# Joining the 64-column runs, and all 512 tokens channels first: one layer of a hybrid encoder on one core

## The chip, the cores and the metric

The kernel runs on one core of a Trainium2 chip. A core has TensorE (PE, matrix products), VectorE (DVE), ScalarE (ACT), GpSimd (POOL) and SyncE (SP, which here only issues transfers), with on-chip memory (SBUF) and accumulators for the products (PSUM, eight banks). The metric is the device time of one execution in microseconds; lower is better.

## The reference

One encoder layer on 512 tokens of 1024 channels. Its first half mixes tokens, its second half is an MLP.

```python
h = rmsnorm(x, pre_mix_norm[l])
proj = h @ w_in[l]
z, xbc, dt_raw, q, k, v, gates = split_cols(proj, IN_SPLITS)
y_ssd = ssd_branch(z, xbc, dt_raw, ...)            # 8 groups of 4 heads, both directions, 4 chunks of 128
y_attn = window_attention(q, k, v, attn_sink[l], rel_bias_table) @ w_attn_out[l]   # 16 heads, +-128 tokens
g = jax.nn.sigmoid((gates + b_gate[l]).astype(jnp.float32))
mixed = (g_ssd * y_ssd + g_attn * y_attn) @ w_o[l]
x = x + rmsnorm(mixed, post_mix_norm[l])
h = rmsnorm(x, pre_mlp_norm[l])
f = jnp.square(jax.nn.relu(h @ w_mlp_in[l])) @ w_mlp_out[l]
x = x + rmsnorm(f, post_mlp_norm[l])
```

`rmsnorm` divides a token's row by the root of its mean square and multiplies each channel by a gain. The row's factor can therefore be applied after a product, since it is one number for each token.

## The kernel before, in words

All data are float32. Most products are made in three parts: a weight `w` and an operand `h` are each split into a high part that TensorE takes in its fast format (fp32r) and a low remainder, and `mm3` adds high x high, high x low and low x high. ScalarE makes the high parts (L513 for weights), GpSimd and VectorE the low ones (L517 for weights, always on GpSimd there). A few products stay in plain fp32.

The program is a list of quanta, each one block of 128 output columns with its weight loads (`cm`, 24 products of 512 columns for a block with 8 parts). Actions between quanta (attention heads, SSD steps) are put at places in that list. All instructions are then recorded and reordered by `Planner`, a list scheduler with a table of costs: it writes a fixed order for each engine, and each engine runs its own queue in that order. A weight tile passes three rings of three buffers: raw (`wr`), high (`wh`) and low (`wl`).

The parts that the change and the prediction touch:

- **The opening** (`start`, `v_quanta`, `start_tokens`, `scale_tokens`). Tokens 0 to 255 come in channels first (`xt`), are multiplied by the gain (`xg`, L685 and L687) and give V and dt by plain products from unnormalised data; the row factor `rst0` is applied when they are taken from PSUM (L617, L618). Tokens 256 to 511 come in token first (`x`), are scaled, transposed by TensorE (L442) and split (L463, L464), and give V and dt by `mm3`. All four blocks of `x` are also read for their sums of squares (L711, L712; L714 and L715 make `rst0`). For tokens 0 to 255 a product of ones with a diagonal of `rst0` (`dg`, L725) spreads the factors over all channels, and L731 to L734 make the split operand `h`. Every later product, K first, reads `h`.
- **Attention** (`attn_scores`, `attn_flip`, `attn_values`). Each head has four blocks of masked scores `P`, their transposes `pT`, and for two heads together 20 products with V whose output fills 64 columns of the array, `ps<-pT,V`.
- **SSD** (`ssd_steps`). For each of 8 groups, `outs(j)` for j = 0 and 1 (two chunks each) makes products of the entering state with C (`ps<-C,pv`), then 8 products of masks with x of 64 columns each (`ps<-m,x`), and merges them on VectorE and GpSimd (L1199 to L1212). `rms` sums squares over channels (`ps<-sh,ones_r`), sends the row through memory and back as a column (`rrow`, `rcol`, `rstd`) and `finish` makes two rows of `yT`.
- **The mixer's output** (`split_y`, `ssd_out_quanta`, `ssd_out_done`, `combine`). 14 of 16 parts of the first two output blocks are multiplied first, and the last two parts, which need the last group, afterwards.

Changing between products of 128 and of 64 columns is a change of TensorE's mode; the planner's `change` knows it, and its `awaited` table lets a 64-column product start only when all that its run needs is ready.

## Time and profile before

| what | value |
|---|---|
| median of 3 runs | 1078.82 us (1078.32 to 1078.97) |
| profiled execution | 1078.3 us, its span 1076.5 us |
| TensorE busy | 1066.9 us, 99% of the span |
| GpSimd, VectorE, ScalarE busy | 798.3, 761.2, 655.5 us |
| granted TensorE clock | 0.998 |
| moved by DMA | 133.21 MB |

The span is the time from the first to the last instruction. In a group of instructions `xN` counts records, and a plain fp32 product leaves two. `out<-in` names the tiles without their buffer numbers. A busy TensorE is not one at its peak, since its instructions overlap and their ends are modelled; starts are the surer reading.

### The profile page before, as it was taken

Reading aid. Unit: us, or ns where it says so; the run is one execution under the profiler, and the core shown is the slowest. Engines: PE = TensorE matmul, PEld = TensorE weight load, DVE = VectorE, ACT = ScalarE, POOL = GpSimd, SP = SyncE. Lnnn points to the kernel's source line nnn. Section 1 sums busy time; section 2 is a strip of 40 time slices with the busy share of each in tenths; the row PEclk is TensorE's granted clock in tenths of the full one; section 3 lists DMA queues with packets and bytes.
Section 4 is the critical chain, followed back from the end, with each engine's and each line's share of the span. In section 5 each row is a group of like instructions: output and inputs, shape, how many; then the busy total and the mean of one; then the engine's idle time right before and its main releaser. Section 6 shows DMA issues by size and latency. Waiting matters only on the chain.

```text
span 1076.5 us, 16682 instructions
## 1 busy us (share of the span) xinstructions
PE 1066.9 (99%) x5542; PEld 895.6 (83%) x5542; DVE 761.2 (71%) x1363; ACT 655.5 (61%) x1409; POOL 798.3 (74%) x991
## 2 busy tenths in 40 slices
PE   9999999999999999999999999999999999999997
PEld 7888888888888888888888888889888888888885
DVE  5777787797787788787778543698663574574698
ACT  7756786777686867676769432456555444444552
POOL 5846558467668899988998965215587898898994
PEclk9999999999999999999999999999999999999999
DMA  8334423433434535243554544317321431424222
GB/s 284 117 101 118 119 81 116 130 101 113 122 112 130 152 113 170 95 151 116 156 140 150 167 146 137 108 52 263 98 69 61 155 98 59 157 94 151 70 98 78
DMA packets 61382, 133.21 MB, mean 124 GB/s; under 512 B 9064, under 2 KB 18792, under 8 KB 61296
## 3 DMA queue, kind: packets, MB, share of 16 engines
q1 hardware_dynamic: 61008, 131.76, 39.3%
q8 instruction: 43, 0.70, 0.3%
q10 hardware_dynamic: 288, 0.39, 0.1%
q14 instruction: 43, 0.35, 0.1%
HBM read 127.63 MB, written 4.49 MB: 123 GB/s over the span
## 4 chain that ended last, share of the span: by engine, by line
PE 96%; DVE 1%; DMA 1%; issue 0%; ACT 0%; POOL 0%; SPq 0%; POOLq 0%; DVEq 0%
PE pp L438 66%; PE ps L438 27%; PE ps L442 3%; DMA wr<-in_wv 1%; PE pp L442 0%; DVE P L940 0%; DVE x L1385 0%; DVE acc L1364 0%; SPq L678 0%; DVE wl L608 0%; DVE ag L1664 0%; DVE h L1372 0%; POOLq L1747 0%; ACT wh L605 0%; POOL mrs L1378 0%
## 5 line engine op out<-in xcount | busy, mean ns | idle before, releaser
L517 POOL TENSOR_TENSOR wl<-wr,wh 128x256 fp32r<-128x256 f32 (+1 forms) x517 | 417.3, 837 | 179.8 <-ACT wh L513 176.4
L438 PE MATMUL pp<-h,wh 128*128 128x512 f32 (+1 forms) x1728 | 525.7, 386 | 0.0
L438 PEld LDWEIGHTS pp<-h,wh 128*128 128x128 f32 x1728 | 318.3, 188 | 61.9 <-issue 1.2
L438 PE MATMUL pp<-h,wl 128*128 128x512 f32 (+1 forms) x864 | 333.7, 386 | 0.0
L513 ACT CAST wh<-wr 128x1024 fp32r<-128x1024 f32 x130 | 135.3, 1041 | 120.6 <-PE pp L438 105.9
L438 PEld LDWEIGHTS pp<-h,wl 128*128 128x128 f32 x864 | 162.6, 188 | 31.8 <-issue 0.2
L1590 POOL TENSOR_TENSOR wl<-wd,wh 128x256 fp32r<-128x256 f32 x158 | 130.7, 864 | 11.8 <-ACT wh L1587 11.8
L1587 ACT CAST wh<-wd 128x512 fp32r<-128x512 f32 x92 | 53.2, 618 | 38.4 <-PE pp L438 19.8
L438 PE MATMUL ps<-wl,fh 128*128 128x512 f32 x184 | 71.8, 390 | 0.0
L438 PE MATMUL ps<-wh,fl 128*128 128x512 f32 x184 | 71.7, 390 | 0.0
L438 PE MATMUL ps<-wh,fh 128*128 128x512 f32 x184 | 71.7, 390 | 0.0
L1425 DVE SCALAR_TENSOR_TENSOR pp<-pp,r 128x256 f32<-128x256 f32 (+1 forms) x31 | 17.3, 559 | 66.1 <-ACT r L1422 65.9
L1168 ACT ACTIVATE n<-cb,tables 128x128 f32<-128x128 f32 x128 | 49.3, 391 | 20.6 <-DVE cb L1159 15.2
L1002 DVE SCALAR_TENSOR_TENSOR u<-pp,cv,u 128x510 f32<-128x510 f32 (+1 forms) x64 | 47.7, 746 | 7.0 <-ACT u L998 5.8
L1169 ACT ACTIVATE m<-cb,tables 128x128 f32<-128x128 f32 x128 | 48.9, 388 | 3.8 <-DVE cb L1159 3.6
L438 PE MATMUL pp<-yl,wh 128*128 128x512 f32 x128 | 49.7, 390 | 0.0
L438 PE MATMUL pp<-yh,wl 128*128 128x512 f32 x128 | 49.7, 389 | 0.0
L438 PE MATMUL pp<-yh,wh 128*128 128x512 f32 x128 | 49.5, 390 | 0.0
L1164 ACT ACTIVATE rf<-rf,tables 128x128 f32<-128x128 f32 x128 | 42.5, 392 | 6.6 <-DMA rf<-csT 6.6
L934 ACT ACTIVATE P<-P,mx 128x384 f32<-128x384 f32 (+1 forms) x64 | 35.2, 553 | 15.9 <-DVE mx L931 15.8
L1204 POOL TENSOR_TENSOR w<-w,E 128x256 f32<-128x256 f32 x48 | 38.7, 820 | 7.6 <-DVE w L1200 6.4
L1100 POOL TENSOR_TENSOR xd<-x,tables 128x256 f32<-128x256 f32 x48 | 32.5, 695 | 15.8 <-ACT x L1025 12.8
(279 smaller groups left out, 2160.1 us busy)
## 6 DMA issues: line engine op xcount, KB each, us to landing
wr<-in_w_in_b SPq DMA_DIRECT2D x74, 512.0 KB, 4.0
wr<-in_w_mlp_in_b SPq DMA_DIRECT2D x32, 512.0 KB, 3.5
wd<-in_w_mlp_out SPq DMA_DIRECT2D x64, 256.0 KB, 4.6
rf<-csT SPq DMA_DIRECT2D x32, 256.0 KB, 4.0
rb<-csT SPq DMA_DIRECT2D x32, 256.0 KB, 4.2
wr<-in_w_ssd_out_b SPq DMA_DIRECT2D x14, 512.0 KB, 3.6
x<-in_x SPq DMA_DIRECT2D x16, 256.0 KB, 5.1
E<-csE SPq DMA_DIRECT2D x32, 128.0 KB, 4.6
```

Source lines behind the costliest of these rows:

```text
L438: self.nc.tensor.matmul(out, lhsT, rhs, start=start, stop=stop, skip_group_check=more)
L513: self.nc.scalar.copy(hi[:, :m], raw)
L517: engines[e].tensor_tensor(lo[:, c], raw[:, c], hi[:, c].bitcast(F32), op=ALU.subtract)
L934: nc.scalar.activation(p[:, :w], p[:, :w], AF.Exp, bias=mx[:, n:n + 1], accum_out=sm[:, n:n + 1])
L1002: nc.vector.scalar_tensor_tensor(u[:, a:e], ps[:, a + d:e + d], self.wtap(t, b), u[:, a:e], op0=ALU.mult, op1=ALU.add)
L1100: nc.gpsimd.tensor_tensor(v4(xd[:, d * 256:(d + 1) * 256]), v4(xs(c)), by_dir(self.coef, c)[:, d].unsqueeze(2).to_broadcast([128, 4, 64]), ...
L1164: nc.scalar.activation(v4(rf)[:, h], v4(rf)[:, h], AF.Identity, bias=ncs[:, 0, h:h + 1])
L1168: nc.scalar.activation(v4(n)[:, h], cb[:, 0], AF.Copy, scale=dt[:, 0, h:h + 1])
L1169: nc.scalar.activation(v4(m)[:, h], cb[:, 1], AF.Copy, scale=dt[:, 1, h:h + 1])
L1204: nc.gpsimd.tensor_tensor(wc, wc, E[:, d], op=ALU.add)
L1587: nc.scalar.copy(hi, src)
L1590: (nc.vector if q == 512 else nc.gpsimd).tensor_tensor(lo[:, c], src[:, c], hi[:, c].bitcast(F32), op=ALU.subtract)
```

## The change

- **All 512 tokens are laid out channels first** in a load of 2 MB (eight tiles of 512 columns). Each is multiplied by the gain and split, without the row factor (`hr`). V and dt of all four token blocks come from these: channel block 0 as a plain product, blocks 1 to 7 by `mm3`, in one pass over the channels with four banks open. The row factor is applied at the eviction of V and dt, for all four blocks. The 16 transposes are gone.
- **K** is computed from `hr` too and scaled at its eviction by the spread row factors `rb`, which are now made for four blocks. The normalised `h` is made afterwards from `xt` and the factors, for the other projections. The `x` tiles now serve only for the sums of squares and are loaded behind `xt` and the V/dt weights; the identity is loaded on SP behind the first K weights.
- **64-column runs are joined.** In SSD groups 3, 4, 6 and 7 the masks' products of j = 0 and 1 stand in one run; attention values (but for the last pair of heads) are held back and put ahead of the next SSD run with j = 1, or j = 0 in the groups that are not joined. The planner takes such a run, and not all products into one bank, as the unit that has to be ready.
- **The mixer**: another order of output blocks, three blocks first in place of two, the later blocks in banks of the other pool, `split_y` in three pieces earlier, the last group's `rms` one quantum later. Score and transpose tiles of the fourth token block share a buffer with others.

```diff
-MIX_ORDER = (0, 4, 1, 5, 2, 6, 3, 7)
+MIX_ORDER, MOST = (0, 4, 2, 6, 1, 5, 3, 7), 3
+SPLIT_Y = ((0, 5, 6), (5, 10, 4), (10, 14, 2))
+Y_BANK = ["ps"] * 8
+PAIRS = (1, 0), (2, 3)
+JOINED = (3, 4, 6, 7)
+ALONE = (7,)
-X_CHUNKS = ((0, 1), (1, 3), (3, 5), (5, 7), (7, 8))
+W_CHUNKS = ((0, 1), (1, 2), (2, 5), (5, 8))
+PLAIN, SCALE_AT = 1, 2.5
-LAST = dict(SCAN, prep=(0, 1, 3, 4), outs=(2.5, 5.5), rms=8, finish=10)
+LAST = dict(SCAN, prep=(0, 1, 3, 4), outs=(2.5, 5.5), rms=9, finish=11)
...
+        def product(k0, k1):
+            def run(parts):
+                if k0 == 0:
+                    banks.extend(self.bank("ps") for _ in range(4))
+                raw, wh, wl = parts[0]
+                for k in range(k0, k1):
+                    for t in range(4):
+                        ps = banks[t][:, :320]
+                        if k < PLAIN:
+                            self.mm(ps, self.xg[k][:, tok(t)], raw[:, k - k0], k == 0, k == 7)
+                        else:
+                            hi, lo = self.hr[k]
+                            self.mm3(ps, (hi[:, tok(t)], lo[:, tok(t)]), (wh[:, k - k0], wl[:, k - k0]), k == 0, k == 7)
+                if k1 == 8:
+                    for t in range(4):
+                        done(t, banks[t])
...
+    def raw_tokens(self):
+        for k, x in enumerate(self.xt):
...
+            hi, lo = self.hr[k]
+            self.split_by(hi, lo, x, g)
+        for t in range(4):
+            xt = self.load_tokens(t)
+            self.token_scale(t, xt)
...
+        self.rb = get("rb")
+        nc.scalar.copy(self.rb, rb)
         for k in range(8):
+            x = self.xt[k]
+            hi, lo = self.h[k]
+            nc.vector.scalar_tensor_tensor(x, x, self.gT[:, k:k + 1], rb, op0=ALU.mult, op1=ALU.mult)
             nc.scalar.copy(hi, x)
+            for e, c in ((nc.vector, slice(0, 512)),) if k % 2 else ((nc.gpsimd, slice(0, 256)), (nc.gpsimd, slice(256, 512))):
+                e.tensor_tensor(lo[:, c], x[:, c], hi[:, c].bitcast(F32), op=ALU.subtract)
...
         def k_done(ps):
+            x = get("kf")
+            nc.vector.tensor_tensor(x, ps, self.rb, op=ALU.mult)
...
         def outs(j):
             def run():
+                off(j)
+                if j == 0 and g in JOINED:
+                    scaled(0)
+                    return
+                while self.due:
+                    self.attn_values(self.due.pop(0))
+                js = (0, 1) if g in JOINED else (j,)
+                for i in js:
+                    diag(i)
+                scaled(j)
+                for i in js:
+                    joined(i)
```

The order of TensorE's queue shows the opening first. Before, the plain products of the second token block (`xg`) are followed by the transposes (`ident,x`; the lines of code are those of the profile):

```order
L438 MATMUL ps_177<-wr_157,xg_116 128x320 x2
L438 MATMUL ps_178<-wr_157,xg_115 128x320
L438 MATMUL ps_178<-wr_157,xg_116 128x320 x2
L442 MATMUL pp_201<-ident,x_205 128x128
L442 MATMUL pp_202<-ident,x_205 128x128
L442 MATMUL ps_203<-ident,x_205 128x128
```

In the changed program (whose lines count 14 more at this place) the queue opens with the warm-up and four plain products, and the three-part products follow at once, one bank after the other:

```order
L452 MATMUL pp_82<-ones_80 128x128 x8
L452 MATMUL ps_229<-wr_142,xg_132 128x320
L452 MATMUL ps_230<-wr_142,xg_132 128x320
L452 MATMUL ps_231<-wr_142,xg_132 128x320
L452 MATMUL ps_232<-wr_142,xg_132 128x320
L452 MATMUL ps_229<-wh_150,hr_109 128x320
L452 MATMUL ps_229<-wl_151,hr_109 128x320
```

Its seam between V and K: the last V product, four products that spread the row factors (`dg`), and then K from `hr` (`pp_434`):

```order
L452 MATMUL ps_232<-wh_162,hr_122 128x320
L452 MATMUL pp_379<-dg_380,ones_80 128x128
L452 MATMUL pp_379<-dg_383,ones_80 128x128
L452 MATMUL pp_379<-dg_386,ones_80 128x128
L452 MATMUL pp_379<-dg_389,ones_80 128x128
L452 MATMUL pp_434<-hr_107,wh_253 128x512
```

Twelve plain products and all transposes have left the queue, 36 three-part products have come, and the factors' products stand ahead of K, where two of them stood inside V.

GpSimd's queue behind the row factors, before: diagonals, K's first weights (`wl_315`), then the low parts of `h`:

```order
L715 TENSOR_TENSOR rst_79<-rst_79,mhalf 128x1
L725 TENSOR_SCALAR dg_262<-ident,rst_79 128x128
L725 TENSOR_SCALAR dg_265<-ident,rst_79 128x128
L517 TENSOR_TENSOR wl_315<-wr_199,wh_314 128x256 x4
L734 TENSOR_TENSOR h_92<-hf_268,h_91 128x256
L734 TENSOR_TENSOR h_94<-hf_268,h_93 128x256
```

The same place in the changed program: both K weight tiles (`wl_254`, `wl_302`), then `h` in turn with the weights of the first Q block (`wl_425`):

```order
L531 TENSOR_TENSOR wl_254<-wr_249,wh_253 128x256 x4
L531 TENSOR_TENSOR wl_302<-wr_251,wh_301 128x256 x4
L742 TENSOR_TENSOR h_92<-xt_124,h_91 128x256 x2
L531 TENSOR_TENSOR wl_425<-wr_299,wh_424 128x256
L742 TENSOR_TENSOR h_96<-xt_126,h_95 128x256 x2
L531 TENSOR_TENSOR wl_425<-wr_299,wh_424 128x256
```

The diagonals have gone to VectorE, `h` stands behind both K tiles, and half of its low parts are VectorE's now.

The last SSD group on TensorE, before: the run of j = 0 between state products, and the run of j = 1, which stands 78 rows later between projections (`pp_6964`):

```order
L438 MATMUL pp_6774<-h_98,wh_6587 128x512
L438 MATMUL pp_6774<-h_97,wl_6588 128x512
L438 MATMUL ps_6792<-C_6456,pv_6603 128x128 x2
L438 MATMUL ps_6795<-m_6618,x_6384 64x128 x4
L438 MATMUL ps_6795<-m_6706,x_6384 64x128 x4
L438 MATMUL ps_6846<-C_6456,B_6361 128x128
```

```order
L438 MATMUL pp_6964<-h_98,wh_6832 128x512
L438 MATMUL pp_6964<-h_97,wl_6833 128x512
L438 MATMUL ps_6985<-m_6850,x_6394 64x128 x4
L438 MATMUL ps_6985<-m_6909,x_6394 64x128 x4
L438 MATMUL pp_6964<-h_99,wh_6832 128x512
```

And in the changed program one run of 16:

```order
L452 MATMUL pp_6982<-h_102,wh_6830 128x512
L452 MATMUL ps_7003<-m_6615,x_6362 64x128 x4
L452 MATMUL ps_7003<-m_6703,x_6362 64x128 x4
L452 MATMUL ps_7012<-m_6848,x_6372 64x128 x4
L452 MATMUL ps_7012<-m_6927,x_6372 64x128 x4
L452 MATMUL pp_6982<-h_101,wl_6831 128x512
```

Both halves now leave the mode once. Over the whole queue, 23 runs of masks and values in the order before are 13 in the changed one, with the same 288 products.

More of the change, by code (lines that the diff above doesn't have):

```diff
@@ L134, in __init__ @@
         self.kind = [self.matmul_kind(n) if e == "PE" else None for n, e in enumerate(self.eng)]
-        self.awaited, banks = {}, {}
+        self.awaited, n0 = {}, None
+        self.runs, last = [], None
         for n, k in enumerate(self.kind):
-            if k and k[1]:
-                banks.setdefault(self.operands(self.ins[n].outs)[0].tensor.name, []).append(n)
-        for bank in banks.values():
-            needed = set().union(*(self.pre[n] for n in bank)) - set(bank)
-            self.awaited.update((n, needed) for n in bank)
+            if k is None:
+                continue
+            if k[1] and last == n0:
+                self.runs[-1].append(n)
+            elif k[1]:
+                self.runs.append([n])
+            n0 = n
+            last = n if k[1] else None
+        for run in self.runs:
+            needed = set().union(*(self.pre[n] for n in run)) - set(run)
+            self.awaited.update((n, needed) for n in run)
     def matmul_kind(self, n):
@@ L648, in run @@
                     self.dt_math()
-            return run
-        return [Quantum([chunk(*c) for c in V_CHUNKS], plain, 0)] + [Quantum([], rest(c), 1) for c in range(3)]
+            return Quantum([chunk(k0, k1)], run)
+        return [product(*c) for c in V_CHUNKS]
     def start(self):
@@ L688, in start @@
-        put(*xt)
-        for t in range(2):
+        self.xt, self.xg = [get("xt") for _ in range(8)], [get("xg") for _ in range(PLAIN)]
+        for k, x in enumerate(self.xt):
+            nc.sync.dma_start(x, self.d_xt[k])
+        self.at(0, self.raw_tokens)
+        self.row = self.const("row", [128, 176])
+        self.sink = self.row[:, 128:144]
+        self.at(1, lambda: self.bcast_row(self.row, self.d_row, 176))
+        self.at(SCALE_AT, lambda: self.scale_tokens(ones))
+        self.at(1, self.later_constants)
@@ L1328, in rest @@
             wh, wl = parts[0]
[L1329 removed]
+            for n, ps in enumerate(banks):
+                m = MIX_ORDER[n] * (MOST - 1) // 4
                 for k in (14, 15):
```

287 lines of the change are left out of this document (119 added, 168 removed).

## The prediction

> **What bounds the kernel now.** I read the engine table and the chain that ended last first, then what TensorE waits for, then its timeline in the opening 25 us and around the 64-column products.
>
> ```profile
> PE 1066.9 (99%) x5542; PEld 895.6 (83%) x5542; DVE 761.2 (71%) x1363; ACT 655.5 (61%) x1409; POOL 798.3 (74%) x991
> PE 96%; DVE 1%; DMA 1%; issue 0%; ACT 0%; POOL 0%; SPq 0%; POOLq 0%; DVEq 0%
> PE pp L438 <- DVE two L663: 1.0, 1, 1.0
> PE ps L442 <- DVE P L940: 0.3, 1, 0.3
> PE ps L438 <- ACT h L463: 0.2, 1, 0.2
> ```
>
> TensorE is the bound from 4.65 us to the end: 96% of the chain is its own work, and all its waits come to 1.5 us, of which 1.0 is the very start. Whatever shortens its stream shortens the run, as long as no operand comes late instead. So the question is what the change takes out of the stream, and which of the four feeding engines then arrives too late.
>
> **The opening.** The timeline of TensorE (start, length, operation, records; a plain fp32 product leaves two records, an fp32r product one):
>
> ```profile
> 4.65 1.97 PE L438 MATMUL ps<-wr,xg 128*128 128x320 f32 x3
> 8.13 1.24 PE L438 MATMUL ps<-wr,xg 128*128 128x320 f32 x4
> 14.91 0.44 PE L442 MATMUL pp<-ident,x 128*128 128x128 f32 x2
> 17.17 0.41 PE L438 MATMUL ps<-wh,h 128*128 128x320 f32 x1 [0.24 <-ACT h L463]
> 19.17 0.46 PE L438 MATMUL ps<-wh,h 128*128 128x320 f32 x2
> 20.05 0.46 PE L438 MATMUL ps<-wh,h 128*128 128x320 f32 x2
> 22.54 0.61 PE L438 MATMUL pp<-dg,ones 128*128 128x128 f32 x4
> 22.90 0.39 PE L438 MATMUL ps<-wl,h 128*128 128x320 f32 x1
> 23.13 0.46 PE L438 MATMUL ps<-wh,h 128*128 128x320 f32 x2
> 25.03 0.62 PE L438 MATMUL pp<-h,wh 128*128 128x512 f32 x2
> ```
>
> Before, 16 plain products run from 4.65 to 14.91, 16 transposes to 17.17, 48 fp32r products and two scale products to 25.03, where K begins. Prices: a plain record starts every (1.97 - 0.90)/2 = 0.53 us at first (0.90 is the longest record of this group) and every (1.24 - 0.43)/3 = 0.27 us later; I put the turn at 7 us. An fp32r product of 320 costs (20.05 - 19.17)/6 = 0.147. Two scale products cost 0.36 before the next start plus 0.23 - 0.147 behind it, 0.45 together.
>
> After: 4 plain products (8 records: five at 0.53 from 4.65, three at 0.27) end at about 8.0. 84 fp32r products are 12.35, so 20.35. Four scale products are 0.9, so 21.25. K then starts **3.7 us** earlier than at 25.03, if nothing is late. What could be late:
>
> ```profile
> 0.00:10.00 10.00, 8.96 (x31) 1.00 0.83 281
> 10.00:20.00 10.00, 9.61 (x51) 1.00 1.05 394
> 4.25 0.35 DVE L687 TENSOR_SCALAR xg<-xt 128x256 f32<-128x256 f32 x1 [3.25 <-DMA xt<-in_xt]
> 11.99 0.63 ACT L711 ACTIVATE junk<-x 128x512 f32<-128x512 f32 x1 [0.34 <-DMA x<-in_x]
> 14.13 0.72 ACT L748 ACTIVATE x<-x,rst 128x512 f32<-128x512 f32 x1
> 19.86 1.10 ACT L513 CAST wh<-wr 128x1024 fp32r<-128x1024 f32 x1
> 637.95 0.70 DVE L1299 SCALAR_TENSOR_TENSOR pp<-gate,pp 128x512 f32<-128x512 f32 x1 [2.91 <-PE pp L438]
> 12.97 0.51 POOL L714 TENSOR_TENSOR rst<-ssq 128x1 f32<-128x1 f32 x1 [1.10 <-DVE ssq L712]
> 13.56 0.54 POOL L715 TENSOR_TENSOR rst<-rst,mhalf 128x1 f32<-128x1 f32 x1
> 21.05 2.83 POOL L517 TENSOR_TENSOR wl<-wr,wh 128x256 fp32r<-128x256 f32 x4 [2.45 <-ACT wh L513]
> ```
>
> The first two rows (last numbers: share of the DMA engines, GB/s) say that the loads run flat out: 2.81 MB in the first 10 us, 0.394 MB per us after. The third x tile lies 3.15 MB into the issue order, so its bytes are through at 10.9; ScalarE got it at 11.99, a lag of 1.1. The changed order of issue is: x channels first and the V/dt weights (3.41 MB together), then the eight x tiles (5.51), the first K weights (6.03), the identity (6.10). By the same rate and lag these land at 12.6, 17.95, 19.3 and 19.45.
> - Each k of the V product now needs a ScalarE split of 512 (0.72), a VectorE one (0.70), and the weight pieces. That is under 1.3 us per k on any engine, where TensorE spends 12 x 0.147 = 1.76 per k. The last k has landed by 12.6 and is split by about 15; it is wanted at 18.6. Hidden by the products themselves. The first xg is ready as before: its first two loads are 0.43 MB where they were 0.46, landed by 4.25.
> - The scale products stand in TensorE's queue ahead of K, so K waits for the last row scale: tile landed 17.95, sum of squares 0.7, GpSimd 0.51 + 0.54, diagonal 0.35, so 20.1, against 20.35. Covered by 0.25 us only; bounds 0 to 1.5, since an error in the landing goes straight through. I take 0, nearest the row of the lag.
> - K's weights: landed 19.3, V's first eviction ahead on ScalarE, cast 1.10, first quarter of the low part 0.71, so about 21.4; wanted by K's third product at 21.7.
> - K from unnormalised parts: 48 products, as many as before; at eviction one VectorE product (0.70 by the row above) more. Nobody on TensorE waits for K until the scores. Zero; bounds 0 to 0.7.
> - The normalised h is wanted by Q at 21.25 + 10.95 = 32.2 (K lasted 25.03 to 35.95 before at this rate, 48 x 0.2275). GpSimd must by then do K's two weight tiles, then h and Q's weights in turn: 20 pieces from 20.6 at 2.83/4 = 0.71 end at 34.8; the last is wanted at 32.2 + 4.5 = 36.7.
>
> ```profile
> 8.05 0.49 DVE L608 TENSOR_TENSOR wl<-wr,wh 128x320 fp32r<-128x320 f32 x1
> 10.66 1.56 DVE L608 TENSOR_TENSOR wl<-wr,wh 128x320 fp32r<-128x320 f32 x2 [0.84 <-ACT wh L605]
> 10.70 1.17 POOL L608 TENSOR_TENSOR wl<-wr,wh 128x320 fp32r<-128x320 f32 x1 [1.44 <-ACT wh L605]
> L517 POOL TENSOR_TENSOR wl<-wr,wh 128x256 fp32r<-128x256 f32 (+1 forms) x517 | 417.3, 837 | 179.8 <-ACT wh L513 176.4
> ```
>
> Beside a GpSimd subtraction two VectorE subtractions took 1.56 instead of 0.98. So at the page's mean of 837 ns, 20 pieces end at 37.3, 0.6 late. Between 0 and 0.9 (four VectorE splits of 0.70 standing in GpSimd's way) I charge **+0.3**, the middle, since both prices occur.
> The Trainium skill (SBUF — State Buffer, section "SBUF: two separate sides") speaks against this part: a VectorE instruction with two SBUF inputs and a GpSimd instruction that reads SBUF exclude each other for the whole instruction. The rows of 1.56 and 1.17 agree with it. By the rule taken strictly the charge is an estimate of 0.9 and the sum below 0.6 worse; by the rows alone it is 0.3.
>
> **The 64-column runs.**
>
> ```profile
> 595.66 0.39 PE L438 MATMUL pp<-h,wl 128*128 128x512 f32 x1
> 595.97 1.09 PE L438 MATMUL ps<-m,x 128*64 128x128 f32 x16
> 597.57 0.39 PE L438 MATMUL pp<-h,wl 128*128 128x512 f32 x1
> 83.34 2.40 PE L438 MATMUL ps<-pT,V 128*64 128x128 f32 x40
> 85.67 1.31 PE L442 MATMUL ps<-ident,P 128*128 128x128 f32 x10
> 136.83 1.06 PE L438 MATMUL ps<-C,pv 128*128 128x128 f32 x8
> 137.81 1.09 PE L438 MATMUL ps<-m,x 128*64 128x128 f32 x16
> 138.84 0.49 PE L438 MATMUL ps<-C,B 128*128 128x128 f32 x2
> ```
>
> A run of 8 lasts 1.03 to the next start, one of 20 lasts 2.33, so a product costs 1.30/12 = 0.108 and leaving the mode 1.03 - 8 x 0.108 = 0.16. Entering: eight records before it should take 0.87 and take 0.98, so 0.11. Among fp32 neighbours a run costs 0.27. Among fp32r neighbours: 595.66 to 597.57 is 1.91, less three products of 0.2275, less 0.87, is 0.36. The order has 23 such runs before and 13 after, so 10 x 0.27 to 10 x 0.36; there are also three changes fewer between fp32 and fp32r, inside that bound. I take **-3.2**, the middle, since both kinds go. All 288 products stay. What is newly behind a wait: the first half of a joined pair stands until the second half's masks are there, and attention values stand until the next SSD run; on VectorE and GpSimd the merge of both halves moves together. They delay only later groups' work, and TensorE's in-order queue has projections in front of each run; cost 0, bounds 0 to 0.5 us at each of 9 changed runs.
>
> **The end of the mixer.** Three output blocks instead of two run 14 of 16 parts first, in banks of the other pool. The work is the same; what hides the last group's row norm changes:
>
> ```profile
> 610.89 0.46 PE ps L438 x2
> 611.35 87.08 PE pp L438 x384
> 618.29 0.38 SPq L1231 DMA_DIRECT2D rcol<-rrow  x1
> 630.58 2.16 DVE L1243 SCALAR_TENSOR_TENSOR yT<-w,cv,rstd 128x256 f32<-128x256 f32 x4 [12.20 <-DMA rstd<-rrow]
> 632.66 2.37 DVE L1291 TENSOR_TENSOR yl<-yT,yh 128x512 fp32r<-128x512 f32 x2
> ```
>
> From the norm's product (611.35) to the last split (635.03) is 23.7 us; the order has 108 products of 0.2268 (24.5 us) in front of the first use before, 94 (21.3 us) after, the low parts some ten products later. But 618.29 is late: SP's queue held three weight loads ahead of the column load, now one plus a load of w_o. Cost between 0 and 2.4; I take 0, as the early part of that chain has at least 2 us to give back. Splitting y earlier moves 14 VectorE and ScalarE splits of under 0.8 beside products that go on anyway: 0.
>
> **The sum.** -3.7 - 3.2 + 0.3 = -6.6. The profiled execution took 1078.3 us (span 1076.5, 1.8 around it); that gives 1071.7. The median of the runs is 1078.82, 0.5 above the profiled one, so on it: 1072.2.
>
> **Rivals.**
> - The opening gains little, because the row scales or K's weights land late: they depend on 6.1 MB of loads, and only 0.25 us of cover stands on the last scale. For: the DMA engines are full (1.05). Against: the rate held for 10 us. With loads 2 to 3 us late the opening gives 1 and the sum is -3.9: 1074.9.
> - The joined runs give nothing, since what the mode change cost comes back as waits for the slower half: only the opening stays, 1075.4. For: the runs now need up to four operands more. Against: 0.5 us of waits outside the start so far.
> - Slower: each of the 9 changed runs stands in TensorE's queue waiting for its last mask, and every projection behind it waits too. Above 6.6/9 = 0.73 us a run the kernel is slower than before; at 1.2 us (a mask is three VectorE passes of 0.70, one half of such a chain late) it is 10.8 lost and 1083 in all. Against: DVE is busy 71%, and before no such run waited.
> - The mode change could turn out hidden and the opening bound by loads at once: no change, 1078.
>
> **How the numbers follow.** Forecast 0.62, with 1070.3 to 1074.3 as its own range: down by the runs at 3.6 (0.4), no charge for GpSimd (0.3), the turn of the plain records two records sooner (0.5) and the profiled time in place of the median (0.5) together; up by the last scale 1.5 late and the charge at 0.9. Little from the opening 0.15, nothing from the runs 0.10, no change 0.05, slower 0.08. A measurement here can tell about 0.2% (2.2 us) from no change: faster is below 1076.7. The first three make faster 0.87; same 0.05; slower 0.08. The range 1070.0 to 1076.2 takes in the first three cases.
>
> **What would show it.** In the new profile K's first product should start near 21.3 and follow the scale products without a gap; 13 runs of 64 columns should stand where there were 23, and a joined run of 16 should last 16 x 0.108 + 0.16; no wait of TensorE over 0.5 us. Wrong would be: a wait on `dg` before 21 us, on `h` near 32 to 37 us, on `m` before a joined run, or on `yl` some 20 us behind the last norm product.

## The result: no gain, and twenty executions spread over 11 us

| | before | changed |
|---|---|---|
| median, 20 executions each | 1078.72 us | 1080.53 us |
| lowest to highest | 1078.08 to 1082.13 | 1074.88 to 1085.84 |
| profiled execution, its span | 1078.3, 1076.5 | 1074.88, 1072.7 |
| VectorE busy | 761.2 us | 775.8 us |

The ratio is 1.0002, 95% interval 0.9987 to 1.0017: the same, where 1072.2 was forecast. (The ratios are worked out from all executions of both kernels, so they differ a little from the quotient of the medians.) The twenty executions fall into two groups: nine between 1074.88 and 1077.81 us, eleven between 1080.44 and 1085.84. The profiled execution happens to be the fastest of all, so its profile alone misleads. Both parts have to be explained: why even this execution gained only 3.8 us of span where 6.6 were expected, and why eleven of twenty executions gained nothing.

The views of the changed kernel's fastest execution that answer to those of before: the engine table, the chain, all waits of TensorE.

```profile
PE 1060.6 (99%) x5542; PEld 893.6 (83%) x5542; DVE 775.8 (72%) x1368; ACT 659.2 (61%) x1408; POOL 799.4 (75%) x991
PE 92%; DVE 4%; DMA 2%; ACT 1%; issue 0%; POOL 0%; SPq 0%; DVEq 0%; POOLq 0%; ACTq 0%
PE ps L452 <- ACT pT L944: 1.7, 1, 1.7
PE ps L452 <- DVE dtw L811: 1.1, 1, 1.1
PE pp L452 <- DVE two L671: 1.0, 1, 1.0
PE ps L452 <- DVE xg L698: 0.2, 1, 0.2
```

VectorE's share of the chain went from 1% to 4%, and two waits are new: for the dt chain (`dtw`) and for a transposed probability tile (`pT`). TensorE's timeline has the landmarks; two rows of before follow behind it, for the same first scores (`KH,Q`) and the first product of the MLP's folded output (`wh,fh`); the rows of before for K and for the first SSD masks (137.81) stand in the prediction.

```profile
19.97 1.16 PE L452 MATMUL pp<-dg,ones 128*128 128x128 f32 x8
20.89 0.71 PE L452 MATMUL pp<-hr,wh 128*128 128x512 f32 x2
43.21 0.28 PE L452 MATMUL ps<-KH,Q 128*128 128x256 f32 x1
45.65 1.15 PE L452 MATMUL ps<-dtw,cst 128*128 128x128 f32 x6 [1.11 <-DVE dtw L811]
77.27 0.44 PE L452 MATMUL ps<-KH,Q 128*128 128x384 f32 x1 [1.67 <-ACT pT L944]
137.25 1.04 PE L452 MATMUL ps<-m,x 128*64 128x128 f32 x16
694.55 0.39 PE L452 MATMUL ps<-wh,fh 128*128 128x512 f32 x1
```

```profile
46.82 0.28 PE L438 MATMUL ps<-KH,Q 128*128 128x256 f32 x1
698.27 0.39 PE L438 MATMUL ps<-wh,fh 128*128 128x512 f32 x1
```

The lead over before is 4.1 us where K starts (25.03 to 20.89), 3.6 at the first scores (46.82 to 43.21), only 0.6 at the first mask products (137.81 to 137.25), and 3.7 at the folded output (698.27 to 694.55). Between these landmarks both kernels run the same products. So the opening did what it should, and between 43 and 137 us the gain was given back: 1.1 + 1.7 us of it in the two waits. (Two of the ten runs saved lie ahead of 137 us, worth some 0.6 us by the prediction's prices, so the loss there is nearer 3.6 us, and 0.8 of it is not accounted for.) The joined runs then earned 3.2 us between 137 and 694.

VectorE and GpSimd in the same execution, from 28 us on (`L742` is the low part of `h`, `L806` seven steps of the dt polynomial, `L531` GpSimd's weight splits):

```profile
28.57 3.24 DVE L742 TENSOR_TENSOR h<-xt,h 128x512 fp32r<-128x512 f32 x3
37.01 4.81 DVE L806 SCALAR_TENSOR_TENSOR dtw<-dtw,dtw 128x256 f32<-128x256 f32 x6
```

```profile
28.22 1.91 POOL L742 TENSOR_TENSOR h<-xt,h 128x256 fp32r<-128x256 f32 x2
35.62 8.38 POOL L531 TENSOR_TENSOR wl<-wr,wh 128x256 fp32r<-128x256 f32 x9
```

VectorE's parts of `h` take 1.05 us each, the polynomial's steps 0.80, and GpSimd's pieces 0.93 where its pace alone is 0.71. In this execution both engines are stretched wherever each subtracts or multiplies two SBUF operands at once. They still overlap in part: from 37.01 to 41.85 VectorE makes six steps and GpSimd some 5.2 pieces, which one after the other at 0.42 and 0.70 us would take 6.2 us and here take 4.84. Now another execution of the same kernel.

### The profile page after: what moved, and what is told of

Same layout as the page of the kernel before. It is cut to its first block, busy times and chain, and to the rows that moved or that the text cites. A ratio compares the mean times of both kernels' runs of the same rounds, so it can differ in the third digit from the quotient of the medians.

```text
span 1072.7 us, 16666 instructions
## 1 busy us (share of the span) xinstructions
PE 1060.6 (99%) x5542; PEld 893.6 (83%) x5542; DVE 775.8 (72%) x1368; ACT 659.2 (61%) x1408; POOL 799.4 (75%) x991
## 4 chain that ended last, share of the span: by engine, by line
PE 92%; DVE 4%; DMA 2%; ACT 1%; issue 0%; POOL 0%; SPq 0%; DVEq 0%; POOLq 0%; ACTq 0%
PE pp L452 58%; PE ps L452 31%; PE ps L456 3%; DMA wr<-in_w_in_b 1%; DMA x<-in_x 1%; DMA xt<-in_xt 1%; DVE dtw L806 1%; DVE xt L739 0%; DMA E<-csE 0%; DVE h L742 0%; POOL wl L531 0%; DVE u L995 0%; DVE P L933 0%; ACT P L927 0%; DVE x L1397 0%
## 5 line engine op out<-in xcount | busy, mean ns | idle before, releaser
L531 POOL TENSOR_TENSOR wl<-wr,wh 128x256 fp32r<-128x256 f32 (+1 forms) x519 | 418.5, 837 | 160.1 <-ACT wh L527 158.1
L452 PE MATMUL pp<-h,wh 128*128 128x512 f32 (+1 forms) x1696 | 514.7, 385 | 0.0
L452 PEld LDWEIGHTS pp<-h,wh 128*128 128x128 f32 x1696 | 312.5, 188 | 60.7 <-issue 0.5
L452 PE MATMUL pp<-h,wl 128*128 128x512 f32 (+1 forms) x848 | 327.5, 386 | 0.1
L527 ACT CAST wh<-wr 128x1024 fp32r<-128x1024 f32 (+1 forms) x130 | 135.3, 1041 | 124.9 <-PE pp L452 92.1
L452 PEld LDWEIGHTS pp<-h,wl 128*128 128x128 f32 x848 | 159.3, 188 | 31.7 <-POOL wl L531 0.7
L1200 POOL TENSOR_TENSOR w<-w,E 128x256 f32<-128x256 f32 x48 | 41.0, 869 | 16.8 <-DVE w L1196 15.8
L1155 POOL TENSOR_TENSOR rb<-rb,tables 128x512 f32<-128x512 f32 x32 | 36.8, 1150 | 7.9 <-DMA rb<-csT 5.8
L1654 DVE TENSOR_TENSOR acc<-acc,ps 128x512 f32<-128x512 f32 x46 | 31.3, 681 | 15.7 <-PE ps L452 15.6
L1163 DVE TENSOR_TENSOR m<-m,n 128x512 f32<-128x512 f32 x32 | 30.1, 941 | 16.3 <-ACT m L1162 15.8
```

Of the source, the lines that this page charges most:

```text
L452: self.nc.tensor.matmul(out, lhsT, rhs, start=start, stop=stop, skip_group_check=more)
L527: self.nc.scalar.copy(hi[:, :m], raw)
L531: engines[e].tensor_tensor(lo[:, c], raw[:, c], hi[:, c].bitcast(F32), op=ALU.subtract)
L1155: nc.gpsimd.tensor_tensor(v4(rb), v4(rb), cs[:, 1].unsqueeze(2).to_broadcast([128, 4, 128]), op=ALU.subtract)
L1200: nc.gpsimd.tensor_tensor(wc, wc, E[:, d], op=ALU.add)
```

## Experiment 1: the changed kernel again, and its two halves

The theory (A) that was put on record: VectorE's longer queue after the opening takes the gain back. The rival (B): the joined runs make the executions differ. Three runs: the changed kernel as it is; with the opening of before; and with nothing joined, the opening kept:

```diff
-JOINED = (3, 4, 6, 7)
-ALONE = (7,)
+JOINED = ()
+ALONE = tuple(range(8))
```

> The changed kernel once more, for the spread of its times. Theory A (VectorE's queue): the opening gives VectorE some 15 us more work in the first 60 us, TensorE waits for it 1 to 2 us near 45 and 76 us, and in a part of the executions these waits are longer or cost TensorE's full clock for some us afterwards: times between 1075 and 1086, granted clock lower in the longer ones. Theory B (the joined runs): waits at joined runs after 120 us make the spread; the trace of a long execution would show them there.

> The joined runs and the mixer's part alone: the opening as before (256 tokens channels first, the others transposed, K from normalised data). Theory A: 10 runs fewer are worth 3.2, so about 1075.5, with a spread under 1 us and no wait of TensorE over 0.5 us. Theory B: the spread of 10 us stays, from about 1075 up.

> The changed opening and the mixer's part with no run joined: every half and every pair of heads by itself. Theory A: 3.2 us more than the changed kernel and the same spread, 1078 to 1089. Theory B: steady near 1075 (before less 3.7).

| | median | lowest to highest | ratio to before |
|---|---|---|---|
| changed kernel again | 1080.44 | 1075.11 to 1082.39 | 1.0008 (0.9994 to 1.0021) |
| opening of before, runs joined | 1074.74 | 1073.76 to 1078.49 | 0.9971 (0.9962 to 0.9980) |
| new opening, nothing joined | 1084.34 | 1078.60 to 1086.16 | 1.0039 (1.0023 to 1.0054) |

Before had 1078.57 beside these. The joined runs (with the mixer's edit) are worth 3.8 us, close to the 3.2 forecast; the opening costs 5.7 us on top of them, and the spread of 7 to 11 us goes with the opening. So B falls as the reason for it. The forecast for the old opening missed in two points: its executions spread over 4.7 us where under 1 was expected (two of ten, at 1077.67 and 1078.49, stand apart), and one wait behind the start was 0.6 us, not under 0.5. The kernel before has such executions too, five of its twenty at 1080.95 to 1082.13; none of these was profiled, and they stay unexplained.

The profiled execution of the repeat took 1081.54 us (span 1079.4). Its long wait is not where theory A put it (1 to 2 us near 45 and 76 us) but earlier, for `h`. First TensorE's greatest wait and its timeline, then its windows (columns: window, its length, busy time and records of TensorE, its weight loads, VectorE, ScalarE and GpSimd, then the granted clock, share of DMA, GB/s).

```profile
PE pp L452 <- DVE h L742: 4.8, 1, 4.8
38.73 0.79 PE L452 MATMUL pp<-h,wh 128*128 128x512 f32 x1 [4.82 <-DVE h L742]
42.31 0.88 PE L452 MATMUL pp<-h,wh 128*128 128x512 f32 x2
```

```profile
36.00:39.00 3.00, 0.27 (x1) 0.27 (x2) 3.00 (x2) 0.00 (x0) 2.13 (x4) 0.50 0.00 0
39.00:42.00 3.00, 3.00 (x8) 2.32 (x9) 2.56 (x6) 1.85 (x5) 0.00 (x0) 0.50 0.37 81
42.00:45.00 3.00, 3.00 (x13) 2.44 (x12) 2.62 (x4) 1.79 (x5) 0.00 (x0) 0.86 0.78 311
```

TensorE stands for 4.8 us, and then runs at half its clock: from 38.73 to 42.31 it starts 8 products, 3.58 us where 8 x 0.2275 is 1.82. (The Trainium skill, "TensorE: Matmul & The Clock Gate", section "What's actually happening", gives half clock after at least one idle window of about 3.4 us. The row of 0.50 agrees on the half; here the clock fell at 36.0, some 2.1 us after the last product had ended.) K starts 1.0 us later than in the first profile, and not because of the row scales: the second tile of `xt` landed late, ScalarE's split of it starts at 7.32 where it started at 5.79, and TensorE waited 0.76 us for that split and 0.23 for VectorE's.

```profile
7.32 1.36 ACT L477 ACTIVATE hr<-xt,gT 128x512 fp32r<-128x512 f32 x2 [1.96 <-DMA xt<-in_xt]
8.09 0.42 PE L452 MATMUL ps<-wh,hr 128*128 128x320 f32 x1 [0.76 <-ACT hr L477]
```

With 0.4 us for a mask these are 4.8 + 1.8 + 1.0 + 0.4 = 8.0; less the 1.1 us wait that this execution does not have, 6.9. The spans differ by 6.7.

VectorE and GpSimd there, over the same place:

```profile
29.20 10.68 DVE L742 TENSOR_TENSOR h<-xt,h 128x512 fp32r<-128x512 f32 x3
40.00 0.68 DVE L742 TENSOR_TENSOR h<-xt,h 128x512 fp32r<-128x512 f32 x1
```

```profile
29.14 1.45 POOL L742 TENSOR_TENSOR h<-xt,h 128x256 fp32r<-128x256 f32 x2
33.32 1.41 POOL L742 TENSOR_TENSOR h<-xt,h 128x256 fp32r<-128x256 f32 x2
34.69 3.44 POOL L531 TENSOR_TENSOR wl<-wr,wh 128x256 fp32r<-128x256 f32 x5
```

This is the reading of the case. Three VectorE subtractions take 10.68 us where 3 x 0.60 are due (a lone one is busy 0.68, and starts follow every 0.60). GpSimd is not stretched at all: its pieces follow each other without a gap, every 0.70, until 38.13. VectorE's three end at 39.88, which is 38.13 and about 3 x 0.60; the first alone lasts 9.48 us, until 38.68 (the first expectation of experiment 3 says 9.2). So VectorE got nothing done until GpSimd's run of pieces ended; such an operation is called held from here on. In the first profile (1074.88 us) the same instructions in the same order took turns. (The Trainium skill, "SBUF — State Buffer", section "SBUF: two separate sides", has an exclusive lock between a VectorE instruction of two SBUF inputs and a GpSimd one that reads SBUF, held for the whole instruction. The held rows agree that they exclude each other; the first profile's, where both overlap in part, agree less. That the waiting engine can be passed over for a dozen instructions the section does not say.)

## Experiment 2: take the second SBUF operand away

From here on theory A is this: GpSimd's run holds VectorE's operation of two SBUF operands. If it is the cause, a VectorE part of `h` that reads one operand from PSUM must be immune. The wait could not be removed alone, so the data were moved:

```diff
-            x = self.xt[k]
+            x = self.bank("ps") if k % 2 else self.xt[k]
-            nc.vector.scalar_tensor_tensor(x, x, self.gT[:, k:k + 1], rb, op0=ALU.mult, op1=ALU.mult)
+            nc.vector.scalar_tensor_tensor(x, self.xt[k], self.gT[:, k:k + 1], rb, op0=ALU.mult, op1=ALU.mult)
```

> The changed kernel, but the four low parts of h that VectorE computes read the scaled tokens from a PSUM bank in place of SBUF, so that each has one operand in SBUF and not two. Theory A (VectorE's subtraction of two SBUF operands is kept waiting by GpSimd's back-to-back splits, and in which executions is chance): VectorE's four low parts take 0.65 to 0.75 us each in every execution, against 1.0 in the changed kernel's fastest profiled execution and 3.6 in the slower one; TensorE doesn't wait for h; the executions agree within 0.4%, median 1073 to 1075.5. Theory B (executions differ for another reason, a clock or a transfer, and the slow subtractions go with it): the executions spread over 1075 to 1086 as before, median 1079 to 1081.

Second, the opposite cure: GpSimd makes all low parts of `h`.

```diff
-            for e, c in ((nc.vector, slice(0, 512)),) if k % 2 else ((nc.gpsimd, slice(0, 256)), (nc.gpsimd, slice(256, 512))):
+            for e, c in ((nc.gpsimd, slice(0, 256)), (nc.gpsimd, slice(256, 512))):
```

> The changed kernel, but all eight low parts of h are computed by GpSimd, none by VectorE. Theory A: nothing of h can be starved on VectorE any more, so the executions agree within 0.5%; but GpSimd has 8 more halves of 0.71 us, 5.7 us, in front of Q's first products, and its last part comes at about 40 us instead of 35.7: TensorE waits for a GpSimd part of h by 1 to 4 us in every execution, median 1075 to 1080. Theory B: spread over 1075 to 1086 whatever computes h.

Third, only the dt chain is moved; fourth, both the first and the third.

```diff
-        w = [self.dtv] + [get("dtw", (128, 4, 64)) for _ in range(5)]
-        v, e, r, s2, p, al = w
+        w = [self.dtv] + [get("dtw", (128, 4, 64)) for _ in range(3)]
+        v, r, p, al = w
+        pb = self.bank("ps").rearrange("p (i c h) -> p i c h", i=2, c=4)
+        e, s2 = pb[:, 0], pb[:, 1]
```

> The changed kernel, but the dt chain keeps e and its square in a PSUM bank: eight of its VectorE operations have one operand in SBUF and not two. The low parts of h stay as in the changed kernel. Theory A: the seven steps of the polynomial take 0.42 us each in place of 0.80 to 0.83 (5.6 us in all becomes 3.0), and the wait of 1.1 us for dtw goes; but the executions still spread, 1074 to 1085, since h is untouched, median 1077 to 1081. Theory B: the same spread; the steps take 0.4 to 0.8.

> Both of these edits: h's VectorE parts and the dt chain each read one operand from PSUM. Theory A: no execution waits for h, the wait of 1.1 us for dtw goes, that of 1.7 us for pT shrinks as VectorE's queue is 2 to 3 us shorter there; the executions agree within 0.4%, median 1071.5 to 1074, below the joined runs alone (1074.7). Theory B: spread and median as the changed kernel, 1079 to 1081.

| | median | lowest to highest | ratio to before |
|---|---|---|---|
| `h` in PSUM | 1073.76 | 1072.87 to 1074.40 | 0.9948 (0.9935 to 0.9961) |
| `h` on GpSimd | 1087.05 | 1080.73 to 1087.73 | 1.0062 (1.0042 to 1.0082) |
| dt chain in PSUM | 1073.98 | 1072.25 to 1080.78 | 0.9968 (0.9948 to 0.9988) |
| both in PSUM | 1078.88 | 1077.31 to 1082.75 | 1.0000 (0.9990 to 1.0011) |

Before had 1078.62 beside these. The first is as theory A said: four parts of 0.6 us, no wait for `h`, and the spread of 11 us gone (six executions within 1.5). Beside GpSimd pieces that follow each other without a gap, VectorE's parts are not stretched at all. It also shows that the hold only found another victim, here a step of the dt chain:

```profile
29.13 1.88 DVE L742 TENSOR_TENSOR h<-ps,h 128x512 fp32r<-128x512 f32 x3
34.63 3.91 DVE L802 TENSOR_TENSOR dtw<-dtw,dtw 128x256 f32<-128x256 f32 x1
34.73 3.53 POOL L531 TENSOR_TENSOR wl<-wr,wh 128x256 fp32r<-128x256 f32 x5
```

`L802` is a step of 0.43 us; it ends at 38.54, GpSimd's run at 38.26. It cost little here: TensorE waited 0.4 us for a scaled Q and 1.0 for K's second eviction behind it.

The second missed: its median lies 7 us above the range. I expected a wait of 1 to 4 us for GpSimd's part of `h`, which came to 0.9; the 11.6 us are something else:

```profile
PE pp L452 <- DVE kf L858: 11.6, 1, 11.6
32.18 11.65 DVE L766 COPY dcol<-row 64x16 f32<-64x16 f32 x1
41.01 2.78 POOL L531 TENSOR_TENSOR wl<-wr,wh 128x256 fp32r<-128x256 f32 x4
```

A copy of 16 columns with one SBUF operand, whose result is first read at 77 us, was held until 43.83, while GpSimd's run lasted until 43.79, and behind the copy in VectorE's queue stood the dt chain, and behind that K's second eviction (at 51.31), for whose bank TensorE waited. So, by this one row, a plain copy from SBUF to SBUF can be held too, not just operations with two operands, and what is lost is decided by what stands behind it. (The same section of the Trainium skill names an fp32 copy from SBUF to SBUF as an operation that locks GpSimd out of the shared ports; the row agrees that the two contend.)

The third: the seven steps take 0.42 us each and the wait for `dtw` is gone, as forecast, while the spread stays (1072.25 to 1080.78), `h` being untouched. One miss: the executions again fall into two groups, six at 1072.3 to 1073.0 and five at 1078.6 to 1080.8 with one between, so that the median, 3 us under the range given, says little.

```profile
36.97 2.68 DVE L808 SCALAR_TENSOR_TENSOR dtw<-dtw,ps 128x256 f32<-128x256 f32 x6
PE ps L452 <- DVE pT L946: 1.5, 1, 1.5
```

The fourth missed by 5 us, and for the reason that explains the others:

```profile
PE ps L452 <- DVE Q L896: 3.0, 1, 3.0
34.24 6.55 DVE L866 TENSOR_TENSOR KL<-kf,KH 64x512 fp32r<-64x512 f32 x1
33.86 6.30 POOL L531 TENSOR_TENSOR wl<-wr,wh 128x256 fp32r<-128x256 f32 x9
```

With `h` and the steps at the head of the dt chain immune, the first operation of two SBUF operands to meet the run of nine pieces is K's low part, which has both operands in SBUF since this change. It is held from 34.24 to 40.79, the run ends at 40.16, and Q's eviction comes 3 us late. All twelve executions lie above 1077.

## Experiment 3: break the run, or leave no victim

Theory A says that the hold ends with GpSimd's run. So first the run is broken: a copy of one column between pieces of `h` and of the first 14 weight tiles, in a chain of data that fixes its place.

```diff
+            if e == "p" and c.start and i < GAPS:
+                self.nc.gpsimd.tensor_copy(lo[:, c.start:c.start + 1], lo[:, c.start - 1:c.start])
             engines[e].tensor_tensor(lo[:, c], raw[:, c], hi[:, c].bitcast(F32), op=ALU.subtract)
...
+                if e is nc.gpsimd and c.start:
+                    e.tensor_copy(lo[:, c.start:c.start + 1], lo[:, c.start - 1:c.start])
                 e.tensor_tensor(lo[:, c], x[:, c], hi[:, c].bitcast(F32), op=ALU.subtract)
```

> The changed kernel with small one-operand copies (128x1) put between GpSimd's pieces of h and of the early weight splits, so that at most three two-operand pieces follow one another there. Theory A (a VectorE operation on two SBUF operands that is caught by a run of GpSimd's back-to-back pieces can be held until that run ends): no VectorE operation between 26 and 46 us lasts more than 2.9 us, a run of three pieces and its own 0.7, against 9.2 in the slower execution of the changed kernel; the longest wait of TensorE for h is under 1.5 us; GpSimd's chain is 2 to 3 us longer; the executions agree within 0.5%, median 1074 to 1077. Rival C (the hold is a fixed stall that a gap does not end): operations of 5 us and more remain, spread and median as the changed kernel, 1079 to 1081.

Then VectorE's parts of `h` and of K are moved, and the small copies of the constant go to ScalarE; at last all three are moved, with the dt chain's last steps in PSUM too. Of these edits only K's, which is new, is printed.

```diff
-            x = get("kf")
+            x = ps
             nc.vector.tensor_tensor(x, ps, self.rb, op=ALU.mult)
```

> The changed kernel with VectorE's parts of h and of K reading one operand from PSUM (K scaled in its own bank), and the two small copies of a constant moved to ScalarE; the dt chain still has two SBUF operands and is the only one left to be held there. Theory A: if an operation is held, it is one of the dt chain, by up to 4 us, until GpSimd's run ends; TensorE doesn't wait for h or kf, at most 1.2 us for dtw; median 1072.5 to 1074.5, agreeing within 0.4%. Rival C: holds of VectorE's h or K parts in PSUM form remain.

> As the one before, and the dt chain's e, its square and dt in a PSUM bank too: between 26 and 46 us VectorE has no operation left with two SBUF operands. Theory A: no VectorE operation there lasts over 0.8 us but the reciprocal (1.75), in any execution; GpSimd's pieces take 0.70 each without a stretch; the executions agree within 0.3%; TensorE's waits before 50 us come to under 1.5 us in all; median 1070.5 to 1073. Rival C: held operations remain, median 1074 to 1080.

| | median | lowest to highest | ratio to before |
|---|---|---|---|
| small copies between | 1077.54 | 1076.98 to 1083.64 | 0.9997 (0.9986 to 1.0009) |
| `h` and K in PSUM | 1075.72 | 1073.87 to 1077.33 | 0.9970 (0.9959 to 0.9981) |
| all three | 1074.12 | 1073.17 to 1077.87 | 0.9964 (0.9952 to 0.9977) |

Before had 1078.79. Breaking the run: in the profile no VectorE operation between 26 and 46 us is held, and the longest of two SBUF operands are those of `h`, 0.96 us from start to start and 1.03 for the last. The price was GpSimd's longer chain, with TensorE waiting 1.8 us for its parts of `h`, in two waits, and the median lies 0.5 above the range. Two of twelve executions still took over 1081 us, which the forecast did not allow; what held them was not profiled. The changed kernel's own first profile had no held operation either, so one profile without a hold proves nothing here: ten of twelve executions within 2.4 us support theory A, no more.

```profile
28.99 2.95 DVE L747 TENSOR_TENSOR h<-xt,h 128x512 fp32r<-128x512 f32 x3
PE pp L453 <- POOL h L747: 1.8, 2, 1.0
```

With `h` and K in PSUM nothing was held in the profile, but the dt chain started 2 us later, behind K's parts (its reciprocal at 35.69, against 33.65 in the changed kernel's fastest execution), and its last steps took turns with GpSimd at 0.84 each: TensorE waited 2.7 us for it. I had allowed 1.2, and the median lies 1.2 above the range. With all three, the stretch up to 50 us is as forecast: polynomial steps of 0.42, no hold, 1.4 us of waits in all, 1.0 of them at the start. The whole run is not: the median lies 1.1 above the range and the executions differ by 0.4%, not 0.3. The profiled execution, the slowest of its six, shows where:

```profile
37.40 3.15 DVE L808 SCALAR_TENSOR_TENSOR dtw<-dtw,ps 128x256 f32<-128x256 f32 x7 [0.33 <-ACT dtw L806]
PE pp L452 <- DVE yl L1301: 2.6, 1, 2.6
L1301 DVE TENSOR_TENSOR yl<-yT,yh x16: 678/1143/6640, 553.3 to 641.9; 128x512 fp32r<-128x512 f32 x16
611.06 6.64 DVE L1301 TENSOR_TENSOR yl<-yT,yh 128x512 fp32r<-128x512 f32 x1 [6.02 <-ACT yh L1300]
611.58 5.58 POOL L531 TENSOR_TENSOR wl<-wr,wh 128x192 fp32r<-128x192 f32 x9
```

In the third row the three numbers are the shortest, median and longest in ns: one of the sixteen low parts of `y` took 6.64 us, and TensorE waited 2.6 us. It ends at 617.70, GpSimd's run at 617.16. The place is another, the hold the same: two SBUF operands beside GpSimd's weight splits.

This can be counted over all fourteen profiled executions of this case. VectorE has just five operations of more than 1.9 us in them: a part of `h` in the repeat (9.48), `L802` with `h` in PSUM (3.91), the copy with `h` on GpSimd (11.65), K's low part with both in PSUM (6.55) and this part of `y`. All five have only SBUF operands, and each ends within 0.7 us of the end of a run of GpSimd pieces.

## Experiment 4: what is left, and the old opening as a control

In the changed kernel a `pT` copy on VectorE or ScalarE keeps TensorE waiting at 75 us. So for heads 0 to 2 ScalarE takes all of them, on top of the three moves to PSUM. And as a control the dt chain alone is moved in the kernel with the old opening.

```diff
-            (self.nc.vector.tensor_copy if n % 2 else self.nc.scalar.copy)(pT[:, :w], pt[:, :w])
+            (self.nc.vector.tensor_copy if n % 2 and h > 2 else self.nc.scalar.copy)(pT[:, :w], pt[:, :w])
```

> The changed kernel with VectorE's parts of h, of K and of the dt chain reading an operand from PSUM, and for heads 0 to 2 all copies of the turned probabilities on ScalarE, where half were on VectorE. Theory A (in the changed kernel VectorE's queue between 26 and 78 us, lengthened by operations that GpSimd holds or stretches, is what takes the opening's gain back): the wait of 1.6 us at 74.5 us for a copy on VectorE goes or falls below 0.8, TensorE's waits before 100 us come to 1.0 to 2.2 us, median 1071.5 to 1073.5. If that wait is ScalarE's as much as VectorE's, it stays at 1.5 us, median 1073 to 1074.5.

> The opening of the kernel before with the joined runs, and only the dt chain's e and its square in PSUM. Theory A: there the chain had slack (TensorE waits for nothing of it although its steps take 0.84 us each), so that shortening it by some 4 us gives nothing: within 0.15% of the joined runs alone, 1073.5 to 1075.5. Rival D (the stretched chain costs in any opening): 1072 to 1073.3, as much as the 1.1 us wait and what follows it in the changed kernel.

| | median | lowest to highest | ratio to before |
|---|---|---|---|
| three moves, `pT` on ScalarE | 1072.89 | 1072.46 to 1073.58 | 0.9943 (0.9929 to 0.9957) |
| old opening, dt chain in PSUM | 1074.33 | 1073.97 to 1074.55 | 0.9957 (0.9944 to 0.9969) |

Before had 1078.46. The control came out as theory A said: shortening the chain (first row below: 0.43 a step) gives 0.4 us against 1074.74, within 0.15%. In the old opening the chain had slack. The kernel before shows how much: the chain's last step ends at 45.86, and TensorE comes to the sums over it at 51.90 (last two rows below, from before). In the changed kernel the chain ends at much the same time, 45.60, but the sums come sooner: the first scores by 3.6 us, and the sums stand 2.4 us behind these (the wait included) where it was 5.1. So the opening made the chain the last to arrive together with the new order of the queue, not alone.

```profile
34.44 2.70 DVE L833 SCALAR_TENSOR_TENSOR dtw<-dtw,ps 128x256 f32<-128x256 f32 x6
PE ps L452 <- DVE mx L920: 1.5, 1, 1.5
PE pp L452 <- DVE dg L731: 1.3, 1, 1.3
```

```profile
45.05 0.81 DVE L824 SCALAR_TENSOR_TENSOR dtw<-tables,row 128x256 f32<-128x256 f32 x1
51.90 1.04 PE L438 MATMUL ps<-dtw,cst 128*128 128x128 f32 x6
```

The second and third rows are waits of the other kernel. It is the best version measured, 0.57% below before, and its median 0.7% below that of the changed kernel (measured in other sets). The median lies in the range, but not by the mechanism I gave, so that is luck: the wait at 75 us stays at 1.5 us (now for a score bank that VectorE has not emptied), and 1.3 us for the last scale are added. Waits before 100 us come to 3.8 us, where 1.0 to 2.2 were forecast. On that wait the second case of the expectation, that it stays at 1.5 us, was right. Whether moving `pT` gained anything against the three moves alone is open: the two ran in different sets, and four of that kernel's six executions were at 1073.2 to 1074.2.

## Why the prediction was wrong

- **K starts 3.7 us earlier, nothing late: right.** In the first profile it starts at 20.89, 0.36 earlier than forecast, and the waits in front, but for the very start, come to 0.2 us. In the second K came 1.0 us later, through the split of the second channel block, which the prediction took to be hidden. The cover of 0.25 us on the last scale was as thin as stated: five other kernels with this opening waited 0.2 to 1.3 us for `dg`.
- **The charge of 0.3 us for the shared work on `h`: wrong, and the step that failed.** It asked when GpSimd would finish with VectorE in its way. GpSimd did finish in time: its 20 pieces ended at about 35.4 us in the second profile, without a stretch. What came late was VectorE's part. I had treated it as the intruder and never as the one to be held, although the pair of rows I quoted (1.56 and 1.17) showed both engines stretched. The bound of 0.9 rested on VectorE's four parts costing their own 0.70 each; three of them took 10.68. With the half clock behind it that one step cost 6.6 us in that execution, the whole of the forecast gain. The sentence on the strict rule of the exclusive lock had the right pair of engines, but its estimate of 0.9 has the same fault: it counts GpSimd's delay only.
- **VectorE's queue behind it: not in the sum at all.** The dt chain and the scores follow `h` on VectorE. The prediction costed each new VectorE operation against TensorE's need for its result, and none against the chain standing behind it. In the first profile the wait for the dt chain's result was 1.1 us. (The other wait, 1.7 us at 75 us for `pT`, is not shown to come from there: it is still 1.6 us with `h`, K and the dt chain all moved.) A row of before showed the price: its polynomial steps already took 0.9 us,

```profile
39.96 1.85 DVE L819 SCALAR_TENSOR_TENSOR dtw<-dtw,dtw 128x256 f32<-128x256 f32 x2
```

  where a 128 x 256 step costs 0.42 with one operand in PSUM. Before, it cost nothing, since TensorE came to the sums only at 51.9 us.
- **K from unnormalised parts, 0 (0 to 0.7): right in the changed kernel**, where K's scores start on time. It also moved K's low part from PSUM to SBUF operands, which the working did not mention and which cost 3.0 us in the run where that part was held.
- **Ten runs fewer, -3.2: right, a little low.** 3.2 us between the landmarks at 137 and 694 us, with two of the ten ahead of them; 3.8 us with the mixer's edit by the halves. No wait for a mask appeared in the first profile, 0.4 us in the second: that rival's place held. The forecast of 1.89 us for a joined run of 16 holds for three of the four (the first starts at 375.63, the next product at 377.52); only the last group's took 2.16 (592.25 to 594.41).
- **The mixer's end, 0: right.** TensorE never waited for `yl` in either profile of the changed kernel; the wait of 2.6 us with all three moved came from a held part of `y`.
- **The rivals.** The kernel ended near the "no change" case, but none of the four named its cause. The list of what would prove the forecast wrong did: a wait for `h` near 32 to 37 us, found at 33.9 to 38.7.

With operands moved, the kernel runs at 1072.9, and in half of the dt run's executions at 1072.3 to 1073.0, close to the forecast of 1072.2. That closeness is partly luck: the two parts saved more than forecast (4.1 us where K starts, 3.8 for the joined runs and the mixer), and waits of 1.5 us and more, which the sum had at nothing, took about the difference. The sum was about right on the work, and wrong about which engine would be kept waiting.

## What stays open

Why one execution takes turns and another holds VectorE for the whole run is not settled: the instructions and their order are the same, and in both VectorE's operation arrived in the middle of a run of pieces. The executions above 1078 us that were not profiled (of the dt run, of the run with small copies, the slowest of the changed kernel) may have other causes. What keeps TensorE waiting at 75 us in most kernels with the new opening is not shown either.

## What to carry to other kernels

When work is moved to or ahead of an engine, ask who is kept waiting on both sides of whatever the two engines share, and what stands in the queue behind the one that loses. Where VectorE and GpSimd both stream from SBUF, give VectorE's operations one operand in PSUM, and all of those that stand beside the run (with two of three moved the kernel gained nothing, 1078.9 us), or expect a delay as long as a whole run of GpSimd pieces. And look at the spread of the executions before believing the profile of one.

## What the runs showed of the hardware that I had not expected

- A VectorE operation of at most 0.7 us on SBUF operands can be held until GpSimd's uninterrupted run ends: 3.91, 6.55, 6.64, 9.48 and 11.65 us in five runs, each ending within 0.7 us of the end of that run; a copy of 64 x 16, which took 0.17 and 0.24 us in the dt run, was one of them.
- The same two instruction streams either take turns (VectorE 1.05 us for 0.68, GpSimd 0.93 for 0.71) or VectorE is held, and which of the two happens differs from one execution to the next of one program: 11 us between executions, against 1.5 us with `h` in PSUM.
- In a wait of 4.8 us without products the granted clock fell to 0.50 some 2.1 us after the last product had ended, and stayed there until some 4.1 us after products had started again, which added 1.8 us to the wait.
